# New model of the transfer queues behind the instruction orders, norm sums of two token chunks on the tensor engine, contiguous token pieces

## The chip, the cores and the metric

The kernel runs on the eight NeuronCores of one Trainium2 chip. Each core works on one sequence of the batch; nothing passes between cores. The metric is the device time of the slowest core, in microseconds (us).

## The reference, cut to what matters

```python
h  = concat([meta, x], axis=1)                  # 16 + 2048 tokens, 2048 channels
xn = rmsnorm(h, norm_g)
v_c, g_c, z_c, u_s, z_s, gl_c, gl_s = split(xn @ w_in)
y_c = silu(layernorm(depthwise_conv31(v_c * sigmoid(g_c)))) * silu(z_c)
y_s = gelu(s5_scan(u_s))                        # complex diagonal recurrence
y_s = y_s * sigmoid(y_s @ w_glu + b_glu) * silu(z_s)
merged = sigmoid(gl_c + b) * (y_c @ w_conv) + sigmoid(gl_s + b) * (y_s @ w_ssm)
out = rmsnorm(h + merged @ w_out, final_g)[:, 16:]
```

## The kernel before

The kernel is written as a list of operations with buffers read and written. A small list scheduler then simulates the five engines and the transfer queues, and the order in which it would start the operations becomes each engine's fixed instruction list. What stands in a list behind a transfer waits with it, so a wrong guess of its landing costs everything behind it: in the kernel before ScalarE sat idle for 13.57 us until a token piece landed, and the tanh behind that piece's square began only at 42.94 us (both are lines in the prediction below). The old model of a transfer shares bytes evenly among busy queues:

```python
    def schedule(self, bw=320e3):
        ...
            if o.dsrc is not None:
                now, left = max(end, ring[e]), float(o.nbytes)
                others = sorted(v for q, v in ring.items() if q != e and v > now)
                while True:
                    rate = min(bw / (1 + len(others)), 0.78 * bw)
                    ...
                ring[e] = end = now + left / rate
                end += 2.2
```

The start: tokens arrive in eight chunks of 258 tokens, four pieces each. A chunk's RMS norm needs squares (ScalarE), their sum over channels (VectorE adds, then a pair of fp32 products with ones), Ln and Exp, and 16 scalings on VectorE. Then TensorE multiplies it with the first four pairs of weights.

```python
        def x_chunk(j):
            px = 2 + j / 100
            for q in range(4):
                t, b = XQ[j % 3][q]
                s_, sB = (part, partB) if q == 0 else sqt[q % 2]
                act(s_, t, AF.Square, n=4 * NC, reads=(b,), writes=(sB,), prio=px)
                if q:
                    tt(part, part, s_, ALU.add, ...)
            ...                                   # one more add, then two fp32 products with ones
            act(r_, ps[bk][:, 0:NC], AF.Ln, ..., prio=px)
            xsq[j] = act(r_, r_, AF.Exp, scale=-0.5, ..., prio=px)
            for k in range(16):
                stt(XMv[:, k, j * NC:(j + 1) * NC], ...)          # scaled tokens, bf16
        ...
        for i in range(PRE_N):                    # PRE_N = 30 groups of dummies
            S.op("pe", [lambda e: e.matmul(ps[7][:, 0:128], ones_b, ones_b, ...)] * 8, 0.8,
                 (CB,), (psB[7],), prio=99, after=(xl[0, 2],))
```

The dummies are meant to keep the clock up; that they do is not shown (the granted clock of the first 72 us was 0.91 with 30 groups in before).

The scan stage (about 160 to 600 us): for each of eight groups of 128 channels, `s5_mats` loads parameters (`par_b`), builds matrices on VectorE, sends one of them through DRAM (`k_scr`); `conv` and `s5_block` read channel-regrouped tokens back from DRAM (`a_scr`, `u_scr`) and run small matmuls between VectorE scans. Projections (lowest priority, 40) fill TensorE between them. After that come gates, branches and the output projection, all wide matmuls. All of `KS`'s writers and readers share one buffer, and the reloads of `c_scr` and `y_scr` are issued without spacing.

Of the kernel before, what the change touches and what calls it, by code (L numbers as in the profile page):

```python
# [12 lines left out]
ALU = mybir.AluOpType  # L13
# [54 lines left out]
class Op:  # L68
    __slots__ = ("eng", "fns", "dur", "deps", "prio", "dsrc", "nbytes", "seq", "ndep", "succ", "ready", "ev",
                 "margin", "clock", "tab")  # L70


class Sched:
# [50 lines left out]
    def schedule(self, bw=320e3):  # L124

        for o in self.ops:
            o.ndep, o.succ, o.ready = len(o.deps), [], 0.0
        for o in self.ops:
            for p in o.deps:
                p.succ.append(o)  # L130
        free = {e: 0.0 for e in self.ENG}
        fut = {e: [] for e in self.ENG}
        rdy = {e: [] for e in self.ENG}
        for o in self.ops:
            if o.ndep == 0:
                heapq.heappush(fut[o.eng], (0.0, o.prio, o.seq, o))
        ring, table = {"sp": 0.0, "act": 0.0, "pool": 0.0}, None
        n = 0
        total = len(self.ops)
        self.finish = 0.0  # L140
        self.log = []
        while n < total:
            best = None
            for e in self.ENG:
                while fut[e] and fut[e][0][0] <= free[e]:
                    _, p, s, o = heapq.heappop(fut[e])
                    heapq.heappush(rdy[e], (p, s, o))
                if rdy[e]:
                    t = free[e]
                elif fut[e]:  # L150
                    t = fut[e][0][0]
                else:
                    continue
                if best is None or t < best[0]:
                    best = (t, e)
            t, e = best
            if not rdy[e]:
                while fut[e] and fut[e][0][0] <= t:
                    _, p, s, o = heapq.heappop(fut[e])
                    heapq.heappush(rdy[e], (p, s, o))  # L160
            _, _, o = heapq.heappop(rdy[e])
            end = t + o.dur
            if o.tab is not None and o.tab != table:
                table = o.tab
                end += 1.3
            free[e] = end
            if o.dsrc is not None:

                now, left = max(end, ring[e]), float(o.nbytes)
                others = sorted(v for q, v in ring.items() if q != e and v > now)  # L170
                while True:
                    rate = min(bw / (1 + len(others)), 0.78 * bw)
                    if not others or now + left / rate <= others[0]:
                        break
                    left -= (others[0] - now) * rate
                    now = others.pop(0)
                ring[e] = end = now + left / rate
                end += 2.2
            else:
                end += 0.2  # L180
            self.order[e].append(o)
            self.log.append((t, o))
            self.finish = max(self.finish, end)
            n += 1
            for q in o.succ:
                r = end + q.margin if e != q.eng or o.dsrc is not None else end
                if r > q.ready:
                    q.ready = r
                q.ndep -= 1
                if q.ndep == 0:  # L190
                    heapq.heappush(fut[q.eng], (q.ready, q.prio, q.seq, q))
# [58 lines left out]
def build():  # L250
# [8 lines left out]
    x_t = din("x_t", [8, 128, 16 * NC])  # L259
# [23 lines left out]
    with es:  # L283
# [75 lines left out]
        def dma(q, pairs, src, nbytes, reads=(), writes=(), **kw):  # L359

            def mk(o, i):
                return lambda e: e.dma_start(out=o, in_=i, allow_slow_non_contiguous=True)  # L362
            return S.op(q, [mk(o, i) for o, i in pairs], (0.55 if q == "sp" else 1.0) * len(pairs), reads, writes,
                        dsrc=src, nbytes=nbytes, **kw)
# [39 lines left out]
        PRE_N = 30  # L404
# [13 lines left out]
        o_th = stl(2 * 1664)  # L418
        o_pw = stl(2 * 64 * POWN * 4)
        o_k = stl(960)  # L420
# [3 lines left out]
        o_t = stl(4800)  # L424
# [63 lines left out]
        def s5t(n):  # L488
            lo = s5o[0]
            s5o[0] += 4 * n  # L490
            assert s5o[0] <= o_t + 4800
            return tile("ST", lo, 4 * n, F32)
# [107 lines left out]
        def x_load(j):  # L600
            for q in range(4):
                t, b = XQ[j % 3][q]
                eng = "act" if j == 0 and q % 2 else "sp"
                xl[j, q] = dma(eng, [(t, x_t[j][:, q * 4 * NC:(q + 1) * 4 * NC])], f"{eng}x{j % 3}{q}", 128 * 16 * NC, (), (b,),
                               prio=0 if j == 0 else 1 + j / 10)

        xsq = {}

        def x_chunk(j):
            px = 2 + j / 100  # L610
            for q in range(4):
                t, b = XQ[j % 3][q]
                s_, sB = (part, partB) if q == 0 else sqt[q % 2]
                act(s_, t, AF.Square, n=4 * NC, reads=(b,), writes=(sB,), prio=px)
                if q:
                    tt(part, part, s_, ALU.add, n=4 * NC, reads=(partB, sB), writes=(partB,), prio=px)
            sm_, smB = ssm[j % 2]
            tt(sm_, part[:, 0:2 * NC], part[:, 2 * NC:4 * NC], ALU.add, n=2 * NC, reads=(partB,), writes=(smB,), prio=px)
            bk = 2 + j % 4
            S.op("pe", [lambda e, i=i: e.matmul(ps[bk][:, 0:NC], ones_f, sm_[:, i * NC:(i + 1) * NC], start=i == 0,  # L620
                                                stop=i == 1) for i in range(2)], 1.2, (onesfB, smB), (psB[bk],), prio=px)
            r_, rB = rst[j % 2]
            act(r_, ps[bk][:, 0:NC], AF.Ln, bias=NORM_EPS, scale=1.0 / D, n=NC, reads=(psB[bk],), writes=(rB,), prio=px)
            xsq[j] = act(r_, r_, AF.Exp, scale=-0.5, n=NC, reads=(rB,), writes=(rB,), prio=px)
            for k in range(16):
                t, b = XQ[j % 3][k // 4]
                stt(XMv[:, k, j * NC:(j + 1) * NC], t[:, (k % 4) * NC:(k % 4 + 1) * NC], PAR["ng"][:, k:k + 1], r_,
                    ALU.mult, ALU.mult, n=NC, reads=(b, rB, psmB), parts=(XB[j][k // 4],), prio=px)
# [20 lines left out]
        for i in range(8):  # L649
            aft = () if i == 0 else (xl[0, 1],) if i == 1 else (xl[i // 2, 2 * (i % 2)],)  # L650
            vgw.append(wload(i, w_main[8 + i], i / 2, after=aft)[:2])
# [3 lines left out]
        assert 12 * NC <= 2 * 1664  # L655
# [13 lines left out]
        def vg_tile(m, j, wg, wgB, wv, wvB, halves=2):  # L669
# [12 lines left out]
            dma("sp", [(a_scr[m][j], pt)], f"pc{pi}", 128 * PCB, (pB,), (ascB[m][j],), prio=5)  # L682
# [6 lines left out]
        def u(m):  # L689
            wv, wB, _ = wnext(m, 28, 2)  # L690
            done = []
            for j in range(8):
# [5 lines left out]
                dma("sp", [(u_scr[m][j], pt[:, 2:NC + 2])], f"pc{pi}", 128 * NC * 2, (pB,), (uscB[m][j],), prio=5)  # L698
# [33 lines left out]
        KS, KSB = tile("ST", o_k, 960)  # L732
        Y2 = [tile("ST", o_y + i * 4096, 4096) for i in range(2)]
        yscB = [Buf() for _ in range(8)]
        KS3 = KS.rearrange("p (x c) -> p x c", x=2)
        S.op("dve", lambda e: e.memset(KS, 0.0), 0.3, (), (KSB,), prio=P5)
# [9 lines left out]
        def s5_mats(m):  # L746

            Q = MATS[m % 2]
            (V, VB), (Vs, VsB), (C, CB_), (Cs, CsB), (Lo, LoB) = Q["V"], Q["Vs"], Q["C"], Q["Cs"], Q["Lo"]
# [57 lines left out]
            for xx in range(2):  # L807
# [5 lines left out]
            dma("sp", [(kd[q], KS3[32 * q + 16:32 * q + 32, :, :]) for q in range(4)], "ks", 64 * 960, (KSB,), (kB,),  # L813
                prio=P5B)
# [3 lines left out]
                f"lo{m % 2}", 128 * 2048, (kB,), (LoB,), prio=P5B)  # L818

        def s5_block(m):  # L820
# [10 lines left out]
            for gp in range(4):  # L831
# [40 lines left out]
                (yscB[m],), prio=10)  # L872
# [10 lines left out]
        def conv(m):  # L883
# [5 lines left out]
            for gp in range(4):  # L889
# [16 lines left out]
                prio=14)  # L906
# [3 lines left out]
        for m in range(8):  # L910
            if m + 1 < 8:
                s5_mats(m + 1)
                u(m + 1)
            if m > 3:
                vg(m)
            conv(m)
            s5_block(m)
        for m in range(8):
            dma("sp", [(CB_t[m][0].rearrange("p (j r) -> p j r", j=8), c_scr[m].rearrange("j p r -> p j r"))], f"cb{m}",
                128 * 4096, (cscB[m],), (CB_t[m][1],), prio=13)  # L920
# [11 lines left out]
        for mm in range(16):  # L932
            wv, wB, _ = wload(mm % 4, w_main[24 + mm], 31)
            for n in range(4):
# [4 lines left out]
                dma("sp", [(z_scr[mm][:, n * 512:(n + 1) * 512], pt)], f"pc{pi}", 128 * 1024, (pB,), (zscB[mm][n],), prio=5)  # L939
# [62 lines left out]
        for m in range(8):  # L1002
            dma("sp", [(YS_t[m][0].rearrange("p (j r) -> p j r", j=8), y_scr[m].rearrange("j p r -> p j r"))], f"ys{m}",
                128 * 4096, (yscB[m],), (YS_t[m][1],), prio=13)
# [92 lines left out]
        for n in range(4):  # L1097
            src = w_out[n // 2].rearrange("p (k t) -> p k t", k=16)[:, :, (n % 2) * 512:(n % 2) * 512 + 512]
            for q in range(4):
                dma("pool", [(WOv[n // 2][:, 4 * q:4 * q + 4, (n % 2) * 512:(n % 2) * 512 + 512], src[:, 4 * q:4 * q + 4, :])],  # L1100
                    f"wo{n}{q}", 128 * 4 * 512 * 4, (), (WOB[n][q],), prio=34,
# [229 lines left out]
def lay_out_x(x, meta):  # L1331

    h = np.concatenate([meta, x], 0).reshape(NC, T, 16, 128)
    return np.ascontiguousarray(h.transpose(1, 3, 2, 0)).reshape(T, 128, 16 * NC)
# [15 lines left out]
```

## Time and profile before

| | before |
|---|---|
| median of the slowest core | 1719.04 us (1715.09 to 1722.15) |
| profiled run, spans of the eight cores | 1695.6 to 1722.4 us |
| TensorE busy | 1639.5 us, 95% |
| main matmul work at full clock, as the prediction counts it | 1595.7 us |
| so lost in the slowest core's span | 126.7 us: 56 before 100 us, 61 in the scan stage, 9.7 in the tail |

The page of the profile, the chain that ended last and the table by stage are shown in the prediction below, with how work is counted. Two more lists carry weight here; a line gives who waited for what, then us in total, how many times, and the longest. Who VectorE (DVE) waited for in the kernel before, the line for the scan parameters:

```profile
DVE CY L324 <- DMA CY<-par_b: 48.5, 6, 17.3
```

And TensorE (PE), lines picked out: the waits that matter in the scan stage (first two) and the start:

```profile
PE ps L350 <- DVE ST L341: 15.3, 3, 8.1
PE ps L350 <- DMA CY<-u_scr: 9.5, 1, 9.5
...
PE ps L350 <- ACT ST L317: 9.5, 4, 4.1
```

L341 is the cast that `KS` needs; it sits behind a par_b wait in VectorE's list, and a convolution matmul waits for the lot.

### The profile page before, as it was taken

Reading aid. Unit: us, or ns where it says so; the run is one execution under the profiler, and the core shown is the slowest. Engines: PE = TensorE matmul, PEld = TensorE weight load, DVE = VectorE, ACT = ScalarE, POOL = GpSimd, SP = SyncE. Lnnn points to the kernel's source line nnn. Section 1 sums busy time; section 2 is a strip of 40 time slices with the busy share of each in tenths; the row PEclk is TensorE's granted clock in tenths of the full one; section 3 lists DMA queues with packets and bytes.
Section 4 is the critical chain, followed back from the end, with each engine's and each line's share of the span. In section 5 each row is a group of like instructions: output and inputs, shape, how many; then the busy total and the mean of one; then the engine's idle time right before and its main releaser. Section 6 shows DMA issues by size and latency. Waiting matters only on the chain.

```text
span 1722.4 us, 25974 instructions; the slowest of 8 cores (1695.6 to 1722.4 us)
## 1 busy us (share of the span) xinstructions
PE 1639.5 (95%) x9568; PEld 932.9 (54%) x9568; DVE 701.0 (41%) x1269; ACT 546.2 (32%) x941; POOL 106.8 (6%) x206
## 2 busy tenths in 40 slices
PE   4899879798999999999999999999999999999997
PEld 4688667687885544444444444444444444444443
DVE  3698347566666510338511112221111221215443
ACT  2555335354445469335211111111111111122222
POOL 1000100000000000000000000000010010100000
PEclk9899989999899999999999999999999999999999
DMA  9742949788658953453544444445555453845722
GB/s 234 175 117 49 159 92 141 119 116 134 124 104 169 221 141 79 98 134 83 124 79 74 74 74 79 81 82 91 94 91 95 86 98 74 166 128 180 239 87 82
DMA packets 115163, 200.86 MB, mean 117 GB/s; under 512 B 19424, under 2 KB 68832, under 8 KB 112864
## 3 DMA queue, kind: packets, MB, share of 16 engines
q0 software_dynamic: 33792, 92.29, 34.7%
q1 hardware_dynamic: 80672, 105.35, 21.5%
q8 instruction: 78, 1.28, 0.3%
q10 hardware_dynamic: 576, 1.58, 0.3%
q14 instruction: 45, 0.37, 0.1%
HBM read 248.92 MB, written 42.53 MB: 169 GB/s over the span
## 4 chain that ended last, share of the span: by engine, by line
PE 83%; DMA 10%; SPq 2%; DVE 2%; ACT 1%; issue 1%; DVEq 0%; ACTq 0%; POOLq 0%
PE ps L350 83%; DMA CY<-par_b 3%; DMA CY<-x_t 3%; SPq L362 2%; DMA a_scr<-ST 2%; DVE CY L324 1%; DMA k_scr<-ST 1%; ACT CY L317 0%; DMA CY<-c_scr 0%; ACT L317 0%; DMA WS<-w_dw 0%; DMA u_scr<-ST 0%; DMA CY<-u_scr 0%; DVE XM L335 0%; PE ps L620 0%
## 5 line engine op out<-in xcount | busy, mean ns | idle before, releaser
L350 PE MATMUL ps<-XM,WS 128*128 128x258 bf16 (+1 forms) x6144 | 1054.6, 330 | 16.5 <-ACT ST L317 8.6
L350 PEld LDWEIGHTS ps<-XM,WS 128*128 128x128 bf16 x6144 | 607.1, 99 | 422.7 <-issue 18.7
L317 ACT ACTIVATE ST<-ps,SM 128x512 f32<-128x512 f32 (+2 forms) x224 | 137.2, 627 | 634.6 <-PE ps L350 634.2
L335 DVE SCALAR_TENSOR_TENSOR ST<-ps,ST 128x512 f32<-128x512 f32 x132 | 91.3, 691 | 528.9 <-PE ps L350 528.9
L350 PE MATMUL ps<-CY,WS 128*128 128x512 bf16 x1280 | 287.0, 379 | 0.0
L350 PEld LDWEIGHTS ps<-CY,WS 128*128 128x128 bf16 x1280 | 125.2, 98 | 151.0
L324 DVE TENSOR_TENSOR CY<-CY 128x257 f32<-128x257 f32 (+3 forms) x192 | 126.0, 671 | 40.1 <-ACT CY L317 19.2
L317 ACT ACTIVATE ST<-ps 128x258 f32<-128x258 f32 (+1 forms) x136 | 65.4, 485 | 164.3 <-PE ps L350 161.4
L317 ACT ACTIVATE CY<-CY 128x514 f32<-128x514 f32 (+2 forms) x104 | 81.5, 797 | 73.2 <-DMA CY<-x_t 32.3
L324 DVE TENSOR_TENSOR CY<-ps,CY 128x514 f32<-128x514 f32 (+2 forms) x97 | 65.3, 680 | 87.4 <-PE ps L350 83.3
L362 POOL DMA_DIRECT2D WS<-w_main x104 | 55.2, 531 | 656.9 <-PE ps L350 474.4
L324 DVE TENSOR_TENSOR CY<-CY,ST 128x512 f32<-128x512 f32 (+3 forms) x115 | 64.2, 592 | 50.6 <-DMA CY<-par_b 48.5
L324 DVE TENSOR_TENSOR ST<-ST 128x512 f32<-128x512 f32 (+3 forms) x87 | 55.3, 648 | 43.9 <-ACT ST L966 27.4
L350 PE MATMUL ps<-ST,WS 128*128 128x256 bf16 x320 | 46.3, 293 | 24.7 <-DVE ST L341 15.3
L350 PE MATMUL ps<-CY 128*128 128x256 bf16 (+1 forms) x320 | 54.5, 281 | 15.8 <-DMA CY<-u_scr 9.5
L340 ACT CAST ST<-ps 128x258 bf16<-128x258 f32 (+1 forms) x96 | 42.1, 442 | 81.8 <-PE ps L350 81.4
L324 DVE TENSOR_TENSOR CY<-ST 128x512 bf16<-128x512 f32 x32 | 21.3, 688 | 95.4 <-DMA ST<-z_scr 75.9
L350 PE MATMUL ps<-XM 128*128 128x512 bf16 (+1 forms) x272 | 56.6, 366 | 0.0
L350 PE MATMUL ps<-CY,XM 128*128 128x512 bf16 x256 | 56.6, 379 | 0.0
L350 PE MATMUL ps<-XM,ST 128*128 128x512 bf16 x256 | 55.4, 379 | 0.0
L350 PE MATMUL ps<-CY,ST 128*128 128x512 bf16 x256 | 55.4, 379 | 0.0
L335 DVE SCALAR_TENSOR_TENSOR XM<-CY,SM,ST 128x258 bf16<-128x258 f32 x128 | 52.3, 479 | 0.0
(80 smaller groups left out, 810.6 us busy)
## 6 DMA issues: line engine op xcount, KB each, us to landing
WS<-w_main POOLq DMA_DIRECT2D x104, 512.0 KB, 7.5
WS<-w_br POOLq DMA_DIRECT2D x32, 512.0 KB, 6.4
CY<-x_t SPq DMA_DIRECT2D x30, 516.0 KB, 12.6
WS<-w_dw POOLq DMA_DIRECT2D x32, 320.0 KB, 8.7
z_scr<-ST SPq DMA_DIRECT2D x64, 128.0 KB, 4.3
ST<-z_scr SPq DMA_DIRECT2D x32, 256.0 KB, 3.6
WS<-x SPq DMA_DIRECT2D x8, 1024.0 KB, 8.6
CY<-x SPq DMA_DIRECT2D x8, 1024.0 KB, 12.3
```

What stands on the lines that cost most here:

```text
L317: f = lambda e: e.activation(out=out_, in_=in_, func=func, bias=bias, scale=scale)
L324: return S.op(eng, lambda e: e.tensor_tensor(out=out_, in0=in0, in1=in1, op=op), d, reads, writes, **kw)
L335: return S.op("dve", lambda e: e.scalar_tensor_tensor(out=out_, in0=in0, scalar=scalar, in1=in1, op0=op0, op1=op1), 0.15 + n / 960.0, read ...
L340: return S.op("act", lambda e: e.copy(out=out_, in_=in_), 0.22 + n / 1200.0, reads, writes, **kw)
L350: return lambda e: e.matmul(a[0], a[1], a[2], start=a[3], stop=a[4])
L362: return lambda e: e.dma_start(out=o, in_=i, allow_slow_non_contiguous=True)
```

## The change

The intent: orders made on a model in which the queues share the engines in proportion to the size of their packets, each queue first in, first out, with store traffic slowing the whole, and a half-clock TensorE after idle windows. These are assumptions of the model. Of them the trace of before shows the half clock (0.50 after waits of 3.82, 4.12 and 8.10 us). With it come norm sums on TensorE for the first two chunks, Ln and Exp ahead of other ScalarE work, later first weights, fewer dummies, a second `KS` buffer, spaced reloads, and token pieces that are contiguous in DRAM. The new model also takes less time for the issue of a transfer (0.45 and 0.55 us, where the old one had 0.55 and 1.0). The diff, cut to its core:

```diff
+        CAP, MIX, ONE = 0.78, 0.45, {"sp": 0.62, "act": 0.62, "pool": 0.76}
+        def rates():
+            heads = [(q, r[0]) for q, r in rings.items() if r]
+            ...
+            out, left, todo = {}, MIX if len(heads) > 1 and any(h[2].store for _, h in heads) else CAP, dict(heads)
+            while todo:
+                tot = sum(h[1] for h in todo.values())
+                ...
+                        out[q] = left * h[1] / tot
@@ dma()
+            pk = packets or 128
+            size = nbytes / pk
+            op.weight = max(15.0, (0.0394 if q == "pool" else 0.0388) * size if size > 700 else 28.0 if size > 400 else 15.0)
+            op.work = pk * op.weight / 16000.0
@@ x_chunk()
+            if j < 2:
+                for q in range(4):
+                    for i in range(2):
+                        act(s_[...half i...], t[...half i...], AF.Square, n=2 * NC, ...)
+                        S.op("pe", [ ...two fp32 products with ones_f, accumulated over the chunk... ], 0.88, ...)
+            else:
+                ...                                # as before
-            act(r_, ..., AF.Ln, ..., prio=px)
-            xsq[j] = act(r_, r_, AF.Exp, ..., prio=px)
+            act(r_, ..., AF.Ln, ..., prio=0.5)
+            xsq[j] = act(r_, r_, AF.Exp, ..., prio=0.5)
@@ elsewhere
-        PRE_N = 30
+        PRE_N = 16
-            aft = () if i == 0 else (xl[0, 1],) if i == 1 else (xl[i // 2, 2 * (i % 2)],)
+            aft = (xl[0, 0],) if i == 0 else (xl[0, 2],) if i == 1 else (xl[i // 2, 2 * (i % 2)],)
-        KS, KSB = tile("ST", o_k, 960)
+        KSs = [tile("ST", o_k + i * 960, 960) for i in range(2)]
+            backs.append(dma("sp", [...], name, 128 * 4096, (b,), (t[1],), prio=13, packets=1024, after=backs[-2:-1]))
-    x_t = din("x_t", [8, 128, 16 * NC])
+    x_t = din("x_t", [8, 4, 128, 4 * NC])
```

## The prediction

> **What bounds the kernel now.** I read the page first, for the busy shares and the slices.
>
> ```profile
> PE 1639.5 (95%) x9568; PEld 932.9 (54%) x9568; DVE 701.0 (41%) x1269; ACT 546.2 (32%) x941; POOL 106.8 (6%) x206
> PE   4899879798999999999999999999999999999997
> DMA  9742949788658953453544444445555453845722
> q0 software_dynamic: 33792, 92.29, 34.7%
> q1 hardware_dynamic: 80672, 105.35, 21.5%
> ```
>
> The tensor engine is the bound, but only from slice 14 on is it full; the first 13 slices (43 us each) have the holes, and there the transfer engines are close to full. The chain that ended last says the same.
>
> ```profile
> 7.83 32.65 DMA CY<-x_t
> 54.78 13.05 DMA CY<-x_t
> 169.09 6.84 DMA CY<-par_b
> 265.06 13.41 DMA CY<-par_b
> 308.69 13.08 DMA CY<-par_b
> 612.49 1100.26 PE ps L350 x5112
> ```
>
> From 612.5 us on the chain is one block of matmuls, 1100.26 / 5112 = 215.2 ns each, without a hole. No order can shorten that block per matmul. After it comes a tail of 9.7 us, which the diff does not touch. So the question is what the first 612.5 us lose. Busy time does not tell it, because it includes dummy matmuls and matmuls at half clock; I count work instead. In the chain's undisturbed piece at 109 us, 168 narrow matmuls took 18.48 us, 110 ns each. The groups by shape, up to 612.4 us, count 3712 narrow ones (256 to 258 columns): 408.3 us; 344 wide ones: 74.0 us; eight norm sums of 0.87 us: 7.0 us; transposes and small products, 0.76 us per group of channels: 6.1 us. That is 495 us of work, so **117 us are lost before 612.5 us**. The table by stage, restricted to the main matmul line, says where:
>
> ```profile
> 0.00:72.00 72.00, 24.98 (x174) 17.93 (x175) 0.91 0.95 222
> 72.00:100.00 28.00, 25.00 (x190) 19.82 (x189) 0.87 0.51 131
> 160.00:240.00 80.00, 61.06 (x509) 51.01 (x507) 0.91 0.75 129
> 240.00:340.00 100.00, 86.62 (x733) 73.55 (x731) 0.92 0.78 118
> 340.00:440.00 100.00, 89.06 (x771) 76.67 (x769) 0.95 0.85 130
> ```
>
> (The columns: stretch, its length, PE busy and count, weight loads, granted clock, transfer share, GB/s.) In 0 to 72 us the 174 matmuls are 19.1 us of work and three norm sums 2.6: **50.3 lost**. 72 to 100: 20.9 + 1.7: 5.4 lost. 100 to 160: none. 160 to 240: 56.0 and 1.5 of small products: 22.5 lost. 240 to 340: 17.9. 340 to 440: 13.7. What is left of the 117, 7.3, lies in 440 to 612. So the start loses about 56 us and the scan stage about 61 us.
>
> The timeline shows the kind of the loss, once in each:
>
> ```profile
> 40.56 1.06 ACT L317 ACTIVATE CY<-CY 128x1032 f32<-128x1032 f32 x1 [13.57 <-DMA CY<-x_t]
> 41.64 1.28 ACT L317 ACT_TABLE_LOAD   x1
> 42.94 0.39 ACT L317 ACTIVATE ST<-ps 128x258 f32<-128x258 f32 x1
> 43.58 1.88 PE L350 MATMUL ps<-XM,WS 128*128 128x258 bf16 x8 [4.12 <-ACT ST L317]
> 321.93 1.63 DVE L324 TENSOR_TENSOR CY<-CY,ST 128x128 f32<-128x128 f32 x3 [9.32 <-DMA CY<-par_b]
> 324.29 1.22 PE L350 MATMUL ps<-ST,WS 128*128 128x256 bf16 x5 [8.10 <-DVE ST L341]
> ```
>
> At 27 us the next entry in ScalarE's list is the square of a token piece that lands only at 40.5; the tanh that would free a bank stands behind it until 42.9 and TensorE fills its time with dummies, then stops. At 312.6 VectorE's next entry needs par_b, and 8 us of TensorE go. These are errors of **order**, not of capacity: the old order was made as if a 256 KB load took 3.3 us (262144 bytes at 0.78 x 320 KB per us, and 2.2), and this one took 13.08.
>
> [...] over the span a q0 packet took 0.347 x 16 x 1722.4 us / 33792 = 283 ns and a q1 packet 0.215 x 16 x 1722.4 / 80672 = 73 ns[...]. That is the new model's weight, and the old one gave equal shares of bytes. [...] The 52 matmuls at 71.8 us, after a wait of 3.8, took 9.32 us, 179 ns each against 110, so a wait costs more than itself. [...] the trace has 1.28 us. Nine of them lie between 41 and 92 us because tanh alternates with the norm's Ln and Exp.
>
> **The change part by part.** *Orders from the new model* change no operation, only when each stands in its engine's list. *Norm sums on TensorE* for the first two chunks: per chunk, three VectorE adds of 1.23 us and one of 0.69 and one pair of fp32 products (0.87 us) go; 16 fp32 products of 0.44 us, 7.0 us, and four more ScalarE calls come. In chunk 0 the last square ended at 16.1 us, VectorE summed until 20.4, the Ln came at 24.1 behind squares of chunk 1, the Exp at 25.4, the scaling at 26.8, the first matmul at 28.6. With sums following the half pieces, Ln and Exp ahead of other ScalarE work, I estimate the product done about 1.4 us after the last square, Ln and Exp 1, scaling of four columns 1.7: first matmul at 20 to 22 us, 7 earlier, if its weights are there (they now wait for the first token piece). In chunk 1 the sums add 7.0 - 0.9 = 6.1 us of work to TensorE, perhaps half of it in holes: 3 lost. *Contiguous pieces* leave rows of 4128 bytes as they were; I give them 0 to 2 us. *Second KS buffer, spaced reloads*: a wait less in the scan stage, small; they share in the middle's sum.
>
> **The start.** In its first 72 us a q1 packet took 0.545 x 16 x 72 / 3635 = 173 ns and a q0 packet 0.360 x 16 x 72 / 1152 = 360 ns. A token chunk of 512 packets is then 5.5 us of all engines, a pair of weights (256 packets) 5.8, either about 6.0 at the measured share of 0.95. Each meeting of a chunk and a pair is 32 matmuls, 3.5 us. From 3 us on, with two items at 15 us, one meeting, four at 27, four meetings, then six at 39, nine, the supply overtakes TensorE early: an ideal start loses about 22 us, against 56 now. I let the new order get half of the 34: **17**.
>
> **The scan stage.** Of its 61 us, waits that TensorE itself shows are 40.6: for DVE ST L341 15.3, u_scr 9.5, w_dw 7.1, DVE CY 6.2 and small ones; the other 20 are the lower clock after them and turns too short to see. The first two, 25, are order alone, since other projections had weights in place. With half of the clock loss, 35; I take a third off for new waits where the model is wrong about a landing: **24 to 25**.
>
> Sum: 17 + 25 - 3 = 39. 1719 - 39 = **1680 us**.
>
> **Rivals.** *The transfers are the start's bound, not the order*: the share of 0.95 up to 72 us speaks for it; against it, TensorE waited 4.1 us for a tanh whose product was long done, and transfers fell to 0.51 afterwards. Then the start gives 5 and the whole is about 1693. *New waits replace the old*: landings of par_b alone ran from 6 to 13 us, so any fixed order is wrong somewhere; list orders are fragile. Then gains of 10 to 15 us: 1705 to 1709. *The scan stage's own chain becomes the bound*: if fillers move forward, its end still decides when the gated branch can start. Against it: gelu was done at 686 us and its first matmul ran at 771, 85 us of slack. This would cost nothing yet. *The model is right almost everywhere*: start 25, middle 40: 1655.
>
> **Range and chances.** The ideal of all this is 1719 - 34 - 61 = 1624, which no static order will reach; the worst I can argue for is a few us over now, by fp32 sums and late first weights. 8 in 10: 1652 to 1708. The line of 2% is 1684.7, close to my centre, so faster 0.54, same 0.42, slower 0.04.
>
> **What would show it.** Right: first main matmul near 20 to 22 us; no tanh more than 2 us behind its product in the first 72 us; over 220 main matmuls in 0 to 72 us; waits of VectorE for par_b (48.5 us in sum) under 20; TensorE's last solid block beginning before 585 us with the same 215 ns. Wrong: as many matmuls in the first 72 us as now (then transfers bound the start), or the same sum of holes before 600 us under other names, or new holes after it, where there are none now.

That queues share by packet was an assumption of mine. What the trace of before shows: ScalarE and VectorE idle for 13.57 and 9.32 us at one transfer each, with the tanh and the cast behind it in their lists (the lines above); a granted clock of 0.50 from 71.8 to 77.5 us after the wait of 3.82, 0.82 from 78 to 81.2 and 1.00 from 81.2 on, and 0.50 too at 43.6 us after 4.12 and at 324.3 after 8.10. The 1.28 us that "the trace has" is one table load; nine of them start between 41.64 and 91.33 us, and by the kernel's list each stands between a tanh and an Ln, in either order.

## More of the kernel before

Most executions agree within some tenths of a per cent (ten of before beside e1: 1710.57 to 1717.54 us). In some executions cores of one die (sometimes of both; a die has four cores) show a lower granted TensorE clock and take 1 to 19% longer (the eleventh: 2010.68 us, with cores 4 to 7 at 0.811 to 0.813 and the others at 0.981 to 0.988); such runs are called slow and are left out here.

Two figures are used below. The **ratio** is the mean time of one kernel's fast runs over the mean time of the kernel before's fast runs of the same rounds on the same chip, so it is not quite the ratio of the quoted medians. The **core mean** is the mean of all eight cores' spans over the fast runs; it scatters less than the slowest core and is compared with the core mean of before on the same chip.

## The result, and the profile after

The changed kernel took **1679.61 us** (median of 4 runs, 1675.88 to 1682.47) against 1720.35 us of before in the same rounds; the ratio is 0.9767, 95% interval 0.9737 to 0.9797. It was run once more on another chip (after_again), beside experiments:

> The kernel after, unchanged, to be compared on one chip with the others of this call. 0.974 to 0.980 of before.

Measured 1670.06 us, 0.9764 (0.972 to 0.9807), a repeat within the range; its interval crosses 0.98, so taken alone it is unclear at a line of 2%.

The page after, the same three rows of busy shares and slices (a slice is now 42 us):

```profile
PE 1631.0 (97%) x9426; PEld 928.3 (55%) x9512; DVE 706.7 (42%) x1262; ACT 554.6 (33%) x954; POOL 106.9 (6%) x206
PE   7999989998999999999999999999999999999997
DMA  9935979889577654443644444445555553837612
```

The first slice rose from 4 to 7 tenths and the holes at slices 5 to 11 are mostly gone, while the transfer engines are a little fuller over slices 5 to 11 than they were. (Some matmul records of the wide shape are missing in this trace, so the count in the first row is low; the narrow ones are complete.) The chain that ended last, in shares of the span, first before, then after:

```profile
PE 83%; DMA 10%; SPq 2%; DVE 2%; ACT 1%; issue 1%; DVEq 0%; ACTq 0%; POOLq 0%
```

```profile
PE 89%; DMA 4%; DVE 2%; SPq 2%; issue 2%; ACT 1%; DVEq 0%; ACTq 0%; POOLq 0%
```

Transfers fell from 10% of the chain to 4%. The table by stage after, with the columns as in the prediction (main matmul line only):

```profile
0.00:72.00 72.00, 35.15 (x301) 28.80 (x302) 1.00 0.98 232
72.00:100.00 28.00, 26.58 (x231) 22.92 (x230) 0.96 0.84 201
160.00:240.00 80.00, 69.24 (x600) 59.15 (x598) 0.96 0.92 132
240.00:340.00 100.00, 96.05 (x853) 82.69 (x852) 0.99 0.92 135
340.00:440.00 100.00, 93.24 (x808) 79.56 (x807) 0.96 0.85 135
```

By the prediction's own count (110 ns each, 0.87 us for a norm sum, 1.5 us of small products per scan row) the losses are now 35.4, 0.9, 12.5, 4.7 and 9.6 us, against 50.3, 5.4, 22.5, 17.9 and 13.7. The whole span lost 1678.5 - 1595.7 = 82.8 us instead of 126.7. Of the 44 us gained on the slowest core, 19 lie before 100 us and 27 in the three scan rows; some 3 us were lost elsewhere. (Before's slowest core and after's are different cores; the mean of all eight is used below.) Transfer shares in the scan rows rose from 0.75 and 0.78 to 0.92.

The waits, after: VectorE for par_b, and TensorE's longest ones, with the `KS` cast last. (The 7.8 us of L725 are the first wait of all, until the first square of a token piece is done.)

```profile
DVE CY L420 <- DMA CY<-par_b: 7.0, 1, 7.0
```

```profile
PE ps L446 <- DMA WS<-w_dw: 8.9, 4, 4.2
PE ps L725 <- ACT CY L413: 7.8, 1, 7.8
PE ps L446 <- DMA CY<-u_scr: 5.7, 1, 5.7
...
PE ps L446 <- DVE ST L437: 1.4, 2, 0.9
```

The median landing time of par_b did not change (9.0 us before, 9.1 after). What changed is who stands behind it: VectorE's wait for it shrank from 48.5 to 7.0 us, and TensorE's wait for the `KS` cast from 15.3 to 1.4. The start, lines picked out of the timeline after (L725 are the norm sums):

```profile
7.77 9.52 PE L725 MATMUL ps<-CY,ST 128*128 128x258 f32 x32 [7.77 <-ACT CY L413]
13.08 0.63 ACT L413 ACTIVATE CY<-CY 128x516 f32<-128x516 f32 x1 [0.73 <-PE ps L725]
17.38 0.39 ACT L413 ACTIVATE ST<-ps 128x258 f32<-128x258 f32 x1 [2.86 <-PE ps L725]
20.21 0.60 PE L446 MATMUL ps<-XM,WS 128*128 128x258 bf16 x4 [1.14 <-DVE XM L431]
26.58 1.28 ACT L413 ACT_TABLE_LOAD   x1 [5.57 <-PE ps L446]
27.88 0.39 ACT L413 ACTIVATE ST<-ps 128x258 f32<-128x258 f32 x1
```

The first main matmul starts at 20.2 us instead of 28.6 (on the mean of the eight cores, 21.3 instead of 29.0). The first tanh now waits for its product, not for a token piece, and runs at 27.9 instead of 42.9: the product ended at 26.5, the table load took 1.28 us, and the tanh began 0.02 us after it (as in before: 42.92 and 42.94).

### The profile page after: what moved, and what is told of

The parts are those of the page before. It is cut to its first block, busy times and chain, and to the rows that moved or that the text cites. A ratio compares the mean times of both kernels' runs of the same rounds, so it can differ in the third digit from the quotient of the medians.

```text
span 1678.5 us, 25748 instructions; the slowest of 8 cores (1665.3 to 1678.5 us)
## 1 busy us (share of the span) xinstructions
PE 1631.0 (97%) x9426; PEld 928.3 (55%) x9512; DVE 706.7 (42%) x1262; ACT 554.6 (33%) x954; POOL 106.9 (6%) x206
## 3 DMA queue, kind: packets, MB, share of 16 engines
q8 instruction: 78, 1.28, 0.3%
## 4 chain that ended last, share of the span: by engine, by line
PE 89%; DMA 4%; DVE 2%; SPq 2%; issue 2%; ACT 1%; DVEq 0%; ACTq 0%; POOLq 0%
PE ps L446 88%; DMA WS<-w_dw 2%; SPq L458 2%; DVE CY L420 1%; DMA WS<-w_main 1%; DMA CY<-x_t 1%; DMA CY<-u_scr 1%; ACT CY L413 0%; DVE CY L431 0%; PE ps L737 0%; ACT L413 0%; DVE XM L431 0%; DVE ST L431 0%; PE ps L725 0%; DVE CY L979 0%
## 5 line engine op out<-in xcount | busy, mean ns | idle before, releaser
L446 PE MATMUL ps<-XM,WS 128*128 128x258 bf16 (+1 forms) x6144 | 1044.0, 329 | 5.9 <-DVE XM L431 2.2
L446 PE MATMUL ps<-CY,WS 128*128 128x512 bf16 x1217 | 282.3, 379 | 3.3
L420 DVE TENSOR_TENSOR CY<-CY 128x512 bf16<-128x512 f32 (+4 forms) x184 | 120.9, 658 | 28.0 <-PE ps L446 11.4
L413 ACT ACTIVATE CY<-CY 128x514 f32<-128x514 f32 (+3 forms) x112 | 82.3, 751 | 55.9 <-DVE CY L420 30.4
L446 PE MATMUL ps<-ST,WS 128*128 128x256 bf16 x320 | 41.9, 281 | 10.5 <-DMA WS<-w_dw 8.9
```

Of the source, the lines that this page charges most:

```text
L413: f = lambda e: e.activation(out=out_, in_=in_, func=func, bias=bias, scale=scale)
L420: return S.op(eng, lambda e: e.tensor_tensor(out=out_, in0=in0, in1=in1, op=op), d, reads, writes, **kw)
L446: return lambda e: e.matmul(a[0], a[1], a[2], start=a[3], stop=a[4])
```

## The experiments

The total was predicted well, so the experiments ask whether it was for the right reasons. My theory: it is the orders, by landing times that are closer to the truth, 24 us in the scan stage and 14 in the start. Rivals: the norm sums and the early start carry it; the contiguous pieces load faster; one part's order is worth nothing without the other's; the sharing by packet is what matters; or any pessimism about landings would do.

Main matmuls done, as the mean of the eight cores of each profiled run (the first column is the start, the next three the scan stage). The first column adds the counts of 0 to 72 and 72 to 100 us, and a matmul across a border counts twice, so it is good to two or three:

| kernel | 0 to 100 us | 160 to 240 | 240 to 340 | 340 to 440 |
|---|---|---|---|---|
| before | 384 | 513 | 739 | 834 |
| after | 528 | 606 | 851 | 850 |
| e1_orders_only | 471 | 664 | 862 | 863 |
| e2_sums_only | 438 | 540 | 771 | 774 |
| e3_layout_only | 411 | 529 | 765 | 827 |
| after_again | 532 | 632 | 865 | 859 |
| e4_no_pe_sums | 513 | 632 | 875 | 890 |
| e16_no_pe_sums_again | 507 | 614 | 837 | 882 |
| e13_sums_one | 512 | 614 | 864 | 889 |
| e9_start_new | 471 | 500 | 793 | 805 |
| e10_scan_new | 388 | 663 | 859 | 867 |
| e14_equal_shares_8 | 556 | 588 | 834 | 845 |
| e15_old_model_slower | 468 | 605 | 854 | 799 |

And the totals:

| kernel | median us | ratio (95%) | core mean less that of before |
|---|---|---|---|
| e1_orders_only | 1673.68 | 0.977 (0.9753 to 0.9787) | -36.3 |
| e2_sums_only | 1718.7 | 1.0018 (0.9992 to 1.0045) | +3.9 |
| e3_layout_only | 1713.29 | 0.9986 (0.9963 to 1.001) | -1.7 |
| e4_no_pe_sums | 1666.4 | 0.973 (0.9712 to 0.9747) | -43.0 |
| after_again | 1670.06 | 0.9764 (0.972 to 0.9807) | -40.0 |
| e9_start_new | 1710.81 | 0.9992 (0.9936 to 1.0047) | -5.0 |
| e10_scan_new | 1683.5 and 1684.0, its fast runs | none given | -26.8 |
| e14_equal_shares_8 | 1677.61 | 0.9749 (0.9711 to 0.9787) | -38.8 |
| e15_old_model_slower | 1691.27 | 0.9825 (0.9778 to 0.9872) | -29.5 |
| e13_sums_one | 1688.17 | 0.9783 (0.9719 to 0.9847) | -43.4 |
| e16_no_pe_sums_again | 1688.7 | 0.9792 (0.9737 to 0.9848) | -42.4 |

(e16's profiled run has two cores at a lower clock, see below.) The core mean of a kernel scattered by 0.4 to 3.0 us (standard deviation) from run to run. The rows come from three chips, each with its own runs of before. All kernels gave correct results.

### e1_orders_only: the new model and nothing else

```diff
-    def schedule(self, bw=320e3):                # the old model
+    def schedule(self, order=None, clock=True):  # the new one, with packets= and store= given to dma() for it
```

> The kernel before with only the new model: no sums on the tensor engine, old token layout, one KS buffer, old priorities, 30 dummies. Theory (orders do it): the scan stage wins its 24 us and the start about half of what it won, so 0.979 to 0.986 of before (1684 to 1696 us). Rival (the sums and the early first matmul carry the gain, orders alone are fragile): 0.99 to 1.00. The first main matmul stays later than 24 us in both.

Measured 0.977, core mean -36.3 us, a little better than the theory's range; the first main matmul at 24.80 us. The orders alone carry the gain. VectorE's wait for par_b was 4.7 us. The rival that the sums carry it falls.

### e2_sums_only: the sums, early Ln and Exp and 16 dummies on the old model

```diff
-            for q in range(4): ... Square, VectorE adds ...
+            if j < 2: ... halves squared, fp32 products on the tensor engine ...
-        PRE_N = 30
+        PRE_N = 16
```

> The kernel before with the old model, plus the sums on the tensor engine for the first two chunks, their Ln and Exp moved forward, and 16 dummies. Theory: the first main matmul comes near 20 to 23 us but is then held by the same head-of-line waits for token pieces, so 0.995 to 1.003. Rival (the sums carry the gain): 0.985 to 0.99. The old model will deal different orders in the scan stage too, so the table by stage is read, not only the total.

Measured 1.0018, core mean +3.9. Here I missed a detail: the first main matmul did not come at 20 to 23 us but at 30.3 on the mean of the eight cores (32.13 in the profiled one). The old model put sums of chunk 1 between the last sums of chunk 0 in TensorE's list. In the profiled core the last square of chunk 0 was done at 18.7 us, but its last two sums stood behind one of chunk 1, whose square was done only at 23.2, and Ln started at 28.75. A sum on the critical engine is one more thing that can be put in the wrong place.

### e3_layout_only: contiguous pieces, all orders identical

```diff
-    x_t = din("x_t", [8, 128, 16 * NC])
+    x_t = din("x_t", [8, 4, 128, 4 * NC])
```

> The kernel before with the token pieces contiguous and nothing else; the orders are identical. Theory: rows stay 4128 bytes, so 0.999 to 1.001 and the same landing times within 1 us. Rival (contiguous pieces load faster and let the start begin earlier): 0.993 to 0.997, first 72 us with over 185 main matmuls instead of 174.

Measured 0.9986 with an interval across 1, core mean -1.7 us. Main matmuls before 100 us rose from 384 to 411, but the profile of before is of another chip, whose runs were 6 to 7 us slower in the core mean. The rival's mark for the start, over 185 main matmuls in 72 us, was met (193 on the mean of the cores, where before had 180), its total was not. A gain of some 2 us is possible and not shown.

### e4_no_pe_sums: after, without the sums

```diff
-            if j < 2:
+            if j < 0:
```

> The kernel after, but the first two chunks' norm sums on VectorE as in the other six. Theory: first main matmul 3 to 5 us later (three adds and the last sum behind the last square), total 3 to 6 us longer than after, so 0.979 to 0.981 of before. Rival 1 (the sums are most of the start's gain): over 10 us longer, 0.983 or more. Rival 2 (the 6 us of extra tensor work for chunk 1 cost as much as the sums win): equal to after, 0.976 to 0.978.

Measured 0.973: faster than e1 on the same chip (their intervals do not meet, and the core mean is 6.7 us lower) and ahead of after's 0.9764, which ran on another chip. I had expected 3 to 6 us longer. The first main matmul came at 21.3 us on the mean of the eight cores, as in after (21.3) and after_again (20.9); the slowest cores' 21.99 and 20.2 are within the scatter of the cores. By 100 us 513 main matmuls were done against 528 and 532, so the sums bring about 2 us into the start by then. But they also put 14 us of fp32 products on TensorE (32 of 0.44; busy 17.0 us in the trace of after), and the last scan row came out ahead here (890 matmuls against 850 and 859; the other two rows are after_again's within 10). A changed start deals new orders further on too, so this comparison alone does not say how much of that is the sums.

### e13_sums_one and e16_no_pe_sums_again: one chunk's sums, none, side by side

```diff
-            if j < 2:
+            if j < 1:        # e13; e16 is e4 again
```

> Sums on the tensor engine for the first chunk alone. The scan stage's orders should be nearly those of the run without sums, so this tells the sums apart from the reshuffle of the scan. Theory: chunk 0's sums run while the tensor engine is idle, first main matmul 1 to 2 us earlier than without, total equal within 3 us: 0.970 to 0.975. Rival (the sums cost what they win even there): 0.975 or more.

> The kernel after without sums on the tensor engine, again, with more rounds, since it came out 0.3% ahead of after. If that holds, 0.972 to 0.9745; if it was the chip, 0.976 to 0.978.

By the slowest core, e13's 0.9783 lies in its rival's range and e16's 0.9792 in neither of its own; both intervals cross 0.98. The cause is in the table by core. In most of their fast runs two neighbouring cores, 4 and 5 or 6 and 7, took 1685 to 1688 us and the other six 1652 to 1670. Here is e16's core 7, then core 5, in a table by stretch (PE, weight loads, DVE, ACT and POOL busy; then granted clock, transfer share, GB/s):

```profile
200.00:240.00 40.00, 40.00 (x304) 32.90 (x303) 8.24 (x15) 9.27 (x23) 1.06 (x2) 0.81 0.78 111
240.00:280.00 40.00, 40.00 (x314) 32.81 (x313) 26.00 (x50) 22.14 (x47) 3.70 (x7) 0.81 0.77 110
```

```profile
200.00:240.00 40.00, 39.75 (x361) 34.72 (x359) 11.88 (x22) 12.07 (x30) 1.06 (x2) 1.00 0.95 125
240.00:280.00 40.00, 38.29 (x356) 33.09 (x355) 30.70 (x60) 24.30 (x52) 3.70 (x7) 1.00 0.92 143
```

On cores 6 and 7 the granted clock was 0.81 from about 200 to 355 us, so a fully busy TensorE did 304 to 317 matmuls in 40 us where the others did 305 to 372, mostly over 345. At 110 ns each the missing ones are some 22 us; these cores ended 27 us after the mean of the other six. Whole dies at this level are in the slow runs that are left out (the 2010.68 us one of before, with cores 4 to 7 at 0.811 to 0.813); here it took a pair, for about 150 us. Elsewhere all eight cores ran wide matmuls without it: in the profiled runs of before and after TensorE was over 99% busy on each core from 640 to 1660 us, at a granted clock of 1.00 and about 215 ns a matmul. I cannot say why the pairs fell in fast runs of this chip and not of the two others. Without that pair the two kernels behave as e4 did: runs in which no pair fell took 1669.86 us (e16) and 1668.36 and 1668.84 (e13). The core means, -43.4 and -42.4, include the late pairs and are equal within their scatter. So **the sums on TensorE win nothing**: none, one or two chunks give -42.4 to -43.0, -43.4 and -40.0 (each with a standard error of 0.6 to 1.5 us; two chunks were never run on one chip with none or one, except in e14 below, -38.8, with other orders). "Equal within 3 us" held; the 1 to 2 us earlier first matmul did not come (21.0 us on the mean of the cores in both). That is the rival of e13's text in substance: the sums cost what they win even there.

### e9_start_new and e10_scan_new: half of the orders each

Both take e1's operations and run both models. Operations made before the first `u` projection are the start, the rest the scan stage and what follows.

```diff
+        S.schedule_old(); old = {e: list(v) for e, v in S.order.items()}
+        S.schedule();     new = {e: list(v) for e, v in S.order.items()}
+        S.schedule(order={e: ([o for o in new[e] if o.seq < cut],        # e10: old
+                              [o for o in old[e] if o.seq >= cut])       # e10: new
+                          for e in S.ENG})
```

> The operations of before. Those of the start (made before the first u projection) stand in the new model's order, those after it in the old model's order; where the two lists meet, an engine takes the start's head first and otherwise the other list's head as soon as the new model has it ready. Theory: the start keeps its 12 us of gain (by the table by stage of the orders-only run), the scan stage keeps its loss: 0.990 to 0.995. Rival (one part's order is worth nothing without the other's): 0.999 to 1.002.

> The reverse: the start in the old model's order, all after it in the new model's. Theory: the scan stage gives most, 25 to 37 us: 0.979 to 0.987, with stage losses of 15 to 27 us between 160 and 440 us and 50 to 56 us before 100 us. Rival as above: 0.999 to 1.002.

e10: its two fast runs, 1683.47 and 1683.96, are 28 us below the mean of before's fast runs (1711.6), the core mean 26.8. Its start (388) is that of before and its scan rows are those of e1. So the scan stage's order is worth about **27 us**. e9: the start is e1's, 471 matmuls by 100 us, 87 more than before, which is 9.6 us of work; the scan rows are as poor as before's. The ratio 0.9992 lies in the rival's range and misses the theory's, but its interval cannot tell -11 from +8 us; the core mean says -5.0 us, with a standard error of about 1.6. On top of the new scan order the start's order is worth 36.3 - 26.8 = 9.5 us, though across two chips. So the start's order gives **5 to 10 us**, and the parts add up roughly. The rival that one is worth nothing without the other is not borne out by the core means, but the verdict for e9 alone is "same".

### e5_equal_shares and e14_equal_shares_8: the share by packet undone

```diff
-                tot = sum(h[1] for h in todo.values())
-                capped = [q for q, h in todo.items() if left * h[1] / tot > ONE[q]]
+                tot = float(len(todo))
+                capped = [q for q, h in todo.items() if left / tot > ONE[q]]
-                        out[q] = left * h[1] / tot
+                        out[q] = left / tot
```

> The kernel after with one thing of the model undone: queues that are busy together share the engines evenly, as the old model had it, and not by packet weight; the work of a transfer, its latency, the cost of stores and the clock stay. Theory of the change's title (the share by packet is what makes the orders good): it gives back 10 us or more, 0.983 or higher. Rival (realistic durations and latencies do it, the share by packet is a detail): within 4 us of after, 0.974 to 0.980.

It took 1970.32 us, a ratio of 1.1509, far outside both. The timeline shows why, and it is not the transfers:

```profile
599.68 28.01 PE L446 MATMUL ps<-XM,WS 128*128 128x512 bf16 x129
627.53 2.40 PE L762 MATMUL ps<-ones_b 128*128 128x128 bf16 x40
629.76 0.82 PE L446 MATMUL ps<-CY 128*128 128x256 bf16 x6
```

L762 are the dummies. They write bank 7, the bank of the scan's output, and have the lowest priority of all. In the start there were holes for 11 of 16 groups; the other five stood behind every projection, until 627 us, and the first scan output (the third line) had to follow them because it writes the same bank. For 400 us the scan stage made no progress and the fillers ran out. So this run says nothing of the share. It shows that dummies without a hole in the start are a danger to what shares their bank; how many fit depends on the order (e1 kept 30 without harm). With 8 groups (`PRE_N = 8`):

> The equal-shares run again without the trap that its trace showed: there the last five groups of dummy matmuls, which write the bank of the scan's output and have the lowest priority, found no hole in the start and stood at 627 us, with the whole scan behind them. Here 8 groups instead of 16, all else equal. Theory of the title (the share by packet matters): loads on the SP queue land later than this model thinks, VectorE waits for par_b 20 us or more again, 0.982 to 0.990. Rival (realistic durations do it, the share is a detail): 0.973 to 0.980.

Measured 0.9749, core mean -38.8, against 0.9764 and -40.0 of after: **equal within the scatter**. VectorE waited 23.8 us for par_b, as the theory had it, but in one wait, and TensorE's waits stayed small (10.1 us the longest, at the start). After_again and e14 ran on different chips and differ by the 8 groups of dummies too; up to that, the share by packet is a detail.

### e15_old_model_slower: the old model made pessimistic

```diff
-    def schedule(self, bw=320e3):
+    def schedule(self, bw=240e3):
-                end += 2.2
+                end += 5.0
```

> The kernel before with its old model, only the two numbers of its transfers made worse: 240 instead of 320 KB per us, and 5.0 instead of 2.2 us to land. If mere pessimism about landings makes good orders, 0.98 to 0.985, with VectorE's wait for par_b under 20 us. If it takes the new model's structure (queues in order behind one another, shares, clock), 0.990 to 1.002.

Measured 0.9825 (unclear at a line of 2%, but a clear gain in the core mean), -29.5. Two numbers of the old model give three quarters of the gain (29.5 of 40; e14 on the same chip has 38.8). But VectorE still waited 34.3 us for par_b. TensorE's wait for the `KS` cast fell to 0.4 us, and the damage came by another path: VectorE's par_b waits of 13.1 and 14.4 us ended at 275.7 and 422.8 us, and just after them, at 278.2 and 424.0, ended waits of TensorE for VectorE of 10.9 and 10.2. (That the sum alone is no measure is shown by e14, where 23.8 us cost TensorE no such wait.) The rest of the gain takes something of the new model's structure (queues in order, cost of stores, issue times, clock) or of the change's other parts; these runs do not part them. Which of the second `KS` buffer, the spaced reloads, the moved Ln and Exp, the later first weights and the fewer dummies contributes was not tried one by one. All of them with the layout, but without the sums, are worth 6.7 us (e4 against e1 on one chip, standard error 0.6); with the sums it is some 4 us (after_again against e1, on different chips).

## Why the prediction was right, and where it was not

**The bound.** Right. The block of wide matmuls is unchanged (215.2 ns each before; after, 4876 weight loads in 1049.3 us from 618.7 on, 215.2 again), and the loss fell from 126.7 to 82.8 us entirely in the parts that were named.

**The kind of loss.** Right: order, not capacity. With all operations as before, e1 alone gives -36.3 us, while the landing time of par_b stays at 9 us.

**The scan stage, 24 to 25 us.** Right in size: 27 on the slowest core's table, 26.8 by e10. The third that was taken off for new waits is not what the traces show: the wait for w_dw rose only from 7.1 to 8.9 us, while of the two waits that were counted as order alone the `KS` cast's fell from 15.3 to 1.4 and u_scr's only from 9.5 to 5.7. That the sum still fits is in part luck.

**The start, 17 less 3.** Right in total, wrong in its split. After_again is 13.2 us ahead of e10 on the same chip in the core mean (-40.0 and -26.8), and what parts them is the start's order with all changes of operations, the second `KS` buffer and the spaced reloads among them. But the order was worth 5 to 10 us, not 17, and the rest was not a loss of 3 us but a gain of some 4 (6.7 without the sums). The half of the gap to an ideal start that I took was a choice, and it was generous; the other gain made up for it by luck.

**The step that failed** is the norm sums: "first matmul at 20 to 22 us, 7 earlier". The time was right, but the sums are not what brought it. On the mean of the eight cores the first main matmul came at 29.0 us before, at 25.5 with new orders alone, at 21.3 and 21.0 with everything but the sums (e4, e16), at 21.0 with chunk 0's sums (e13) and at 21.3 and 20.9 with both (after, after_again). So the sums' term was nothing within the scatter, not 7. The prediction had the product done 1.4 us after the last square; it was done 2.9 us after: the products took 9.5 us (the L725 line above), where 16 of 0.44 make 7.0. And the squares now waited for products (0.73 us in the same lines), so that the last square ended 3.1 to 3.5 us after the fourth token piece landed, against 1.9 without the sums. From that landing to Ln it is 5.9 to 6.3 us with the sums and 6.2 to 6.6 without.

What did move the first matmul are two other things, not tried one by one: the fourth token piece landed at 12 us instead of 14.7 (14.8 in e1, 14.1 with the contiguous pieces alone, so the later first weights are the likely cause), and Ln came 4.3 to 4.7 us after the last square (e4, e16) where it had come 7.6 after, behind squares of chunk 1. The products' cost on TensorE took back what the sums brought later in the start, or more: -42.4 to -43.4 without them or with one chunk's, -40.0 with two, on different chips.

**The reason behind the model.** I leaned on the share by packet (a q0 packet of 283 ns beside a q1 packet of 73; these means show how long packets took, not how the engines are shared). It was not needed: e14 shares evenly and is as fast. Later landing times are the larger part, as e15 shows with the old model: by its formula 256 KB then take 6.4 us instead of 3.3; par_b took 9.0 in the median before and 6.6 in e15.

**The rivals.** "Transfers are the start's bound" is partly right: the share was 0.98 in the first 72 us and the start's order gave less than I took. "New waits replace the old" did not come to any size (in the scan stage w_dw rose by 1.8 us). "The scan's own chain becomes the bound" did not come.

**The signs.** First main matmul at 20.2 us (foretold 20 to 22); 301 main matmuls in 72 us (over 220); par_b wait 7.0 us (under 20); TensorE full from 540 us on, 71.9 of 72 us busy (before 585). These held. One did not quite: matched by the kernel's own lists and the semaphore times in the trace, eight of the nine tanhs in the first 72 us began 0.1 to 1.8 us after their product ended (in before up to 8.8), but the one at 55.75 us began 4.0 us after, behind a norm's Ln and Exp and two table loads. That the others held is not proof of each cause: the sums' part shows it.

A version that may beat both kernels is after without the sums (e4): 0.973 on an undisturbed chip. Where a pair of cores lost its clock it was 0.9792, and it never ran beside after on one chip, so its lead over after is small and not shown.

## What to carry to other kernels

Where engines take fixed lists, a transfer whose landing is guessed 6 us too early (par_b: 3.3 us in the old model, 9.0 in the median and up to 13.4 in the chain of before) costs the engines behind it, not itself: read which engine waits in whose list, and make the order with landing times measured under load, before refining how queues share. Count matmuls per stage instead of busy time, and compare means over all cores. Give low-priority helper work, such as dummies, a buffer of its own, or it can hold the whole schedule back (256 us in the core mean, e5).
